# A transformer kernel whose pool of weight buffers is laid from the upper end of the on-chip memory downwards

## The chip, the cores and the metric

The kernel runs on one core of a Trainium2 chip. The metric is the device time in microseconds (us) of one execution; it is measured in several runs, and their median counts. A profile of one more execution shows what each engine did: TensorE (PE, matmuls; its weight loads are shown apart as PEld), VectorE (DVE), ScalarE (ACT), GpSimd (POOL), SyncE (SP, which issues most DMAs) and the DMA engines, which move data between the chip's large memory and the on-chip memory that the engines work from.

## What is computed

The reference takes 256 tokens of width 1024 through three layers: an HGRN2 layer (a gated linear recurrence) and a banded attention layer, each with a SwiGLU feed-forward of width 2816 and with modulation by a conditioning vector, and then a layer with four kinds of attention heads and a convolutional feed-forward of width 4096. Cut to what matters:

```python
c_act = silu(c)
for layer in range(2):
    sh1, sc1, g1, sh2, sc2, g2 = split(c_act @ mod_w[layer] + mod_b[layer], 6)
    u = rms_norm(h, norm_mix[layer]) * (1 + sc1) + sh1
    mix = hgrn2_mixer(u, ...) if layer == 0 else chunk_band_attention(u, k_pad, v_pad, ...)
    h = h + g1 * mix
    u = rms_norm(h, norm_ffn[layer]) * (1 + sc2) + sh2
    h = h + g2 * swiglu(u, ffn_w_in[layer], ffn_w_out[layer])
    if layer == 0:
        k_pad, v_pad = shared_kv(h, c_act, ...)
x = rms_norm(h, final_norm)
h = rms_norm(x, attn_pre_norm)
mix = concat(moba(h), nsa(h), diff(h), swa(h))
x = x + rms_norm(mix @ w_out, attn_post_norm)
x = x + rms_norm(conv_ffn(rms_norm(x, ffn_pre_norm), ...), ffn_post_norm)
```

All of it is in float32, and some 240 MB of weights are each read once. So nearly all the work is large matrices times 256 token columns.

## The kernel before

**Weights.** Every weight matrix is cut into units of at most 128 x 1088 numbers. A unit is loaded by SP into a tile `w_raw` (`emit_dma`, L186; 7 such buffers). The units of the large projections are then split in two: ACT writes the rounded part `w_hi` (L193), and DVE writes the rest `w_lo` = `w_raw` - `w_hi` (L195), 4 buffers each. The conditioning vectors' matrices are used from `w_raw` as they are. All three tiles come from the pool `wts`. `pump` issues each load as soon as the buffer that it needs was read for the last time, so the loads run ahead of the matmuls by up to seven units.

**Matmuls.** The activations are split in the same way into a high and a low tile. `mm3` multiplies high by high, high by low and low by high into one accumulator (L258, L259, L260):

```python
PE.matmul(o, lhsT=whi, rhs=xhi, ...)   # L258
PE.matmul(o, lhsT=whi, rhs=xlo, ...)   # L259
PE.matmul(o, lhsT=wlo, rhs=xhi, ...)   # L260
```

The first operand (`lhsT`, 128 x 128) is loaded into the array ahead of its matmul, and the second (`rhs`) streams through it. In most projections the weights are loaded and 256 columns of activations stream (`lin_A`, `lin_At`, `acc_pairs`). In `lin_B` and `down_B` it is the other way round: the activations are loaded and 512 columns of weights stream. The split activations lie in the eight large slots `s0` to `s7` of the pool `big` (all shown as `s` in the profile), with one exception: the output projection of the first layer (`a_w_out`, 175 to 201 us) reads them from the tiles `ohi` and `olo` of that phase's own pool (`hg_o`, L966, and `hg_ol`, L971). Its 192 matmuls use the same function `acc_pairs` and the same weight tiles as the other output projections.

**Order.** The order of all work is written out by hand (`HG_ORDER`, `L1_ORDER`, `B2_ORDER` and the order of the steps), under `tc.manual_schedule()`.

**Memory.** Tiles get their places from pools that stand one behind the other: `cst` (constants), `big` (the slots), `wts`, `wk` (small work tiles: `sq`, `nt`, `sig`, `rstd`, ...), and behind `wk` one pool for each phase in turn (`hg`, `mid`, `b2`: `ohi`, `olo`, `att`, `pt`, `bias`, ...), the next taking the place of the last:

```python
cst = ctx.enter_context(tc.tile_pool(name="cst", bufs=1))
big = ctx.enter_context(tc.tile_pool(name="big", bufs=1))
wts = ctx.enter_context(tc.tile_pool(name="wts", bufs=1))
wk = ctx.enter_context(tc.tile_pool(name="wk", bufs=2))
```

Of the kernel before, what the change touches and what calls it, by code (L numbers as in the profile page):

```python
# [131 lines left out]
def kernel(ctx: ExitStack, tc: tile.TileContext, x, c, mod_w, mod_b, norm_mix, norm_ffn,  # L132
# [10 lines left out]

    cst = ctx.enter_context(tc.tile_pool(name="cst", bufs=1))
    big = ctx.enter_context(tc.tile_pool(name="big", bufs=1))
    wts = ctx.enter_context(tc.tile_pool(name="wts", bufs=1))
    wk = ctx.enter_context(tc.tile_pool(name="wk", bufs=2))
    phase = {}
    ps = ctx.enter_context(tc.tile_pool(name="ps", bufs=1, space=bass.MemoryType.PSUM))
# [1742 lines left out]
```

## Time and profile before

| what | value |
|---|---|
| median of 3 runs | 1158.81 us (1157.78 to 1161.32) |
| the profiled execution's own time | 1159.24 us |
| its span, from the first to the last instruction | 1157.4 us |
| PE busy / PEld busy | 1116.8 us (96%) / 1035.9 us (89%) |
| DVE / ACT / POOL busy | 763.6 us (66%) / 573.7 us (50%) / 140.0 us (12%) |
| SP's DMA queue, share of 16 DMA engines | 64.3% |

The busy time of PE is a sum of instructions that overlap: a matmul is shown from its start to its modelled end, and the next one starts before that. So what a matmul costs is read from the distance between two starts, not from its duration. The time around the span (1159.24 - 1157.4 us) is not in the profile.

### The profile page before, as it was taken

Reading aid. Unit: us, or ns where it says so; the run is one execution under the profiler, and the core shown is the slowest. Engines: PE = TensorE matmul, PEld = TensorE weight load, DVE = VectorE, ACT = ScalarE, POOL = GpSimd, SP = SyncE. Lnnn points to the kernel's source line nnn. Section 1 sums busy time; section 2 is a strip of 40 time slices with the busy share of each in tenths; the row PEclk is TensorE's granted clock in tenths of the full one; section 3 lists DMA queues with packets and bytes.
Section 4 is the critical chain, followed back from the end, with each engine's and each line's share of the span. In section 5 each row is a group of like instructions: output and inputs, shape, how many; then the busy total and the mean of one; then the engine's idle time right before and its main releaser. Section 6 shows DMA issues by size and latency. Waiting matters only on the chain.

```text
span 1157.4 us, 23598 instructions
## 1 busy us (share of the span) xinstructions
PE 1116.8 (96%) x9689; PEld 1035.9 (89%) x9689; DVE 763.6 (66%) x1237; ACT 573.7 (50%) x913; POOL 140.0 (12%) x201
## 2 busy tenths in 40 slices
PE   6988999999999999999999999999998999999997
PEld 5985789899999979888999999988888999999997
DVE  3586765877777587885564454667766766766666
ACT  3355454644344566565443443746555544544454
POOL 4044410000000001250000000013312100000000
PEclk9989999999999999999999999999999999999999
DMA  9966776888888776865766556673342656555551
GB/s 278 332 236 201 225 227 224 277 285 294 291 282 290 224 239 226 286 238 172 229 194 207 183 172 167 158 217 110 110 146 77 217 181 199 178 180 189 187 178 55
DMA packets 176124, 241.92 MB, mean 209 GB/s; under 512 B 18712, under 2 KB 142160, under 8 KB 176016
## 3 DMA queue, kind: packets, MB, share of 16 engines
q1 hardware_dynamic: 174928, 239.54, 64.3%
q8 instruction: 76, 1.25, 0.4%
q0 software_dynamic: 912, 0.81, 0.3%
q14 instruction: 32, 0.26, 0.1%
q10 hardware_dynamic: 176, 0.07, 0.0%
HBM read 239.33 MB, written 1.05 MB: 208 GB/s over the span
## 4 chain that ended last, share of the span: by engine, by line
PE 83%; DVE 7%; ACT 4%; DMA 3%; issue 2%; POOL 1%; SPq 0%; DVEq 0%; ACTq 0%; POOLq 0%
PE pb_b L258 14%; PE pb_b L260 14%; PE pb_b L259 14%; PE pb_acc L258 10%; PE pb_acc L260 10%; PE pb_acc L259 10%; DVE w_lo L195 2%; ACT w_hi L193 2%; DMA w_raw<-in_kv_w_dram 1%; DMA w_raw<-in_a_w_in_dram 1%; PE pb_b L463 1%; PE pb_b L1216 1%; PE pb_gv L524 1%; DVE nt L573 1%; DMA w_raw<-in_mod_w_dram 1%
## 5 line engine op out<-in xcount | busy, mean ns | idle before, releaser
L195 DVE TENSOR_TENSOR w_lo<-w_raw,w_hi 128x1024 fp32r<-128x1024 f32 (+1 forms) x335 | 409.2, 1245 | 178.2 <-ACT w_hi L193 171.0
L258 PE MATMUL pb_b<-s,w_hi 128*128 128x256 f32 x1488 | 424.7, 285 | 5.1 <-ACT s L1750 2.9
L260 PE MATMUL pb_b<-s,w_lo 128*128 128x256 f32 x1488 | 422.0, 284 | 1.5 <-DVE w_lo L195 1.4
L259 PE MATMUL pb_b<-s,w_hi 128*128 128x256 f32 x1488 | 422.9, 284 | 0.4
L193 ACT CAST w_hi<-w_raw 128x1024 fp32r<-128x1024 f32 (+1 forms) x336 | 342.1, 1045 | 78.9 <-DMA w_raw<-in_a_w_in_dram 16.1
L258 PEld LDWEIGHTS pb_b<-s,w_hi 128*128 128x128 f32 x1488 | 285.9, 192 | 12.5 <-issue 3.8
L260 PEld LDWEIGHTS pb_b<-s,w_lo 128*128 128x128 f32 x1488 | 286.0, 192 | 2.4 <-DVE w_lo L195 2.3
L259 PEld LDWEIGHTS pb_b<-s,w_hi 128*128 128x128 f32 x1488 | 286.0, 192 | 1.9 <-DVE s L585 0.7
L258 PE MATMUL pb_acc<-s,w_hi 128*128 128x256 f32 x656 | 190.4, 290 | 0.2 <-ACT w_hi L193 0.2
L260 PE MATMUL pb_acc<-s,w_lo 128*128 128x256 f32 x656 | 186.9, 285 | 2.8 <-DVE w_lo L195 2.8
L259 PE MATMUL pb_acc<-s,w_hi 128*128 128x256 f32 x656 | 186.6, 284 | 0.0
L258 PEld LDWEIGHTS pb_acc<-s,w_hi 128*128 128x128 f32 x656 | 126.9, 193 | 5.4 <-issue 3.7
L260 PEld LDWEIGHTS pb_acc<-s,w_lo 128*128 128x128 f32 x656 | 126.8, 193 | 3.4 <-DVE w_lo L195 3.4
L259 PEld LDWEIGHTS pb_acc<-s,w_hi 128*128 128x128 f32 x656 | 127.0, 194 | 0.2
L1209 POOL TENSOR_SCALAR att<-att,sm 128x128 f32<-128x128 f32 (+1 forms) x72 | 46.7, 666 | 631.9 <-DVE sm L1202 348.0
L1063 ACT CAST s<-sig 128x512 fp32r<-128x512 f32 x38 | 23.6, 622 | 121.1 <-DVE sig L1073 121.1
L258 PE MATMUL pb_acc<-w_hi,s 128*128 128x512 f32 x192 | 77.4, 403 | 1.7 <-ACT s L579 1.0
L259 PE MATMUL pb_acc<-w_lo,s 128*128 128x512 f32 x192 | 75.6, 394 | 0.8 <-DVE w_lo L195 0.8
L260 PE MATMUL pb_acc<-w_hi,s 128*128 128x512 f32 x192 | 75.5, 393 | 0.0
L1776 ACT ACTIVATE sig<-att,vb_t,vc_t 128x256 f32<-128x256 f32 x32 | 17.6, 596 | 77.4 <-DVE att L1771 77.4
L1069 ACT ACTIVATE sig<-pb_b 128x512 f32<-128x512 f32 x22 | 13.2, 598 | 79.7 <-PE pb_b L260 79.7
L1786 POOL TENSOR_TENSOR sig<-sig,rstd 128x512 f32<-128x512 f32 x16 | 22.7, 1417 | 240.1 <-ACT sig L1784 240.1
(373 smaller groups left out, 1259.2 us busy)
## 6 DMA issues: line engine op xcount, KB each, us to landing
w_raw<-in_mod_w_dram SPq DMA_DIRECT2D x96, 512.0 KB, 4.9
w_raw<-in_ffn_w_in_dram SPq DMA_DIRECT2D x88, 512.0 KB, 5.1
w_raw<-in_ffn_w_out_dram SPq DMA_DIRECT2D x44, 512.0 KB, 4.7
w_raw<-in_a_w_in_dram SPq DMA_DIRECT2D x32, 512.0 KB, 5.2
w_raw<-in_ffn_w_gate_dram SPq DMA_DIRECT2D x32, 512.0 KB, 3.7
w_raw<-in_ffn_w_up_dram SPq DMA_DIRECT2D x32, 512.0 KB, 5.0
w_raw<-in_ffn_w_down_dram SPq DMA_DIRECT2D x32, 512.0 KB, 3.6
w_raw<-in_kv_mod_w_dram SPq DMA_DIRECT2D x16, 512.0 KB, 5.6
```

The costliest lines, as they stand in the source:

```text
L193: SC.copy(hi, raw)
L195: DV.tensor_sub(lo, raw, hi.bitcast(F32))
L258: PE.matmul(o, lhsT=whi, rhs=xhi, start=start, stop=False, skip_group_check=True)
L259: PE.matmul(o, lhsT=whi, rhs=xlo, start=False, stop=False, skip_group_check=True)
L260: PE.matmul(o, lhsT=wlo, rhs=xhi, start=False, stop=stop, skip_group_check=True)
L463: PE.matmul(st[:, 0:256], lhsT=mean_d, rhs=sq[:, 256 * m:256 * m + 256], start=j == 0 and m == 0, stop=j == n - 1 and m == 1)
L524: PE.matmul(g[32 * j:32 * j + 32, 0:256], lhsT=by, rhs=r, start=start, stop=stop, tile_position=(0, 32 * j))
L1063: SC.copy(hi, hid)
L1069: SC.activation(sg, g, AF.Silu)
L1209: GP.tensor_scalar(t[:, i, cs], t[:, i, cs], r[:, 2 * b + i:2 * b + i + 1], 1.0, op0=OP.mult, op1=OP.mult)
L1776: SC.activation(zm, am, AF.Identity, bias=vcol("conv_b")[:, f:f + 1], scale=vc_t[:, 64 + f:65 + f])
L1786: GP.tensor_mul(zp, zp, rs_pair())
```

## The change

The pool `wts` is laid from the upper end of the memory downwards. All other pools stay on the lower side, so `wk` and the phases' pools, which stood behind `wts`, now stand right behind `big`.

```diff
-    wts = ctx.enter_context(tc.tile_pool(name="wts", bufs=1))
+    wts = ctx.enter_context(tc.tile_pool(name="wts", bufs=1, side="right"))
     wk = ctx.enter_context(tc.tile_pool(name="wk", bufs=2))
```

The two built programs have the same instructions in the same order with the same waits on every engine; only addresses differ. These are the addresses (bytes within a partition) and what is left of them after division by 256. A buffer of `wts` is 4352 = 17 x 256 bytes, so all buffers of the pool have the same remainder.

| tile | before | remainder | after | remainder |
|---|---|---|---|---|
| `s0` to `s7` | 30720 to 96256 | 0 | the same | 0 |
| `w_raw`, first of 7 | 96256 | 0 | 164064 | 224 |
| `w_hi`, first of 4 | 126720 | 0 | 194528 | 224 |
| `w_lo`, first of 4 | 144128 | 0 | 211936 | 224 |
| `sq`, first of `wk` | 161536 | 0 | 96256 | 0 |
| `ohi`, first of 4 | 209952 | 32 | 144672 | 32 |
| `olo`, first of 4 | 218144 | 32 | 152864 | 32 |
| `flip` (constant of the bias steps) | 181664 | 160 | 116384 | 160 |
| `late` (constants) | 25440 | 96 | 25440 | 96 |

All tiles of `wk` and of the phases move down by 65280 = 255 x 256 bytes and keep their remainders. The tiles of `wts` move up by 67808 bytes.

## Rows read from the trace of the kernel before

**Rows 1.** The page: busy us, share of the span and instructions of each engine.

```profile
PE 1116.8 (96%) x9689; PEld 1035.9 (89%) x9689; DVE 763.6 (66%) x1237; ACT 573.7 (50%) x913; POOL 140.0 (12%) x201
```

**Rows 2.** The page: the chain of waits that ended last, by engine and by line.

```profile
PE 83%; DVE 7%; ACT 4%; DMA 3%; issue 2%; POOL 1%; SPq 0%; DVEq 0%; ACTq 0%; POOLq 0%
PE pb_b L258 14%; PE pb_b L260 14%; PE pb_b L259 14%; PE pb_acc L258 10%; PE pb_acc L260 10%; PE pb_acc L259 10%; DVE w_lo L195 2%; ACT w_hi L193 2%; DMA w_raw<-in_kv_w_dram 1%; DMA w_raw<-in_a_w_in_dram 1%; PE pb_b L463 1%; PE pb_b L1216 1%; PE pb_gv L524 1%; DVE nt L573 1%; DMA w_raw<-in_mod_w_dram 1%
```

**Rows 3.** The page's costliest groups: xcount, then busy us, mean ns, idle before.

```profile
L258 PE MATMUL pb_b<-s,w_hi 128*128 128x256 f32 x1488 | 424.7, 285 | 5.1 <-ACT s L1750 2.9
L260 PEld LDWEIGHTS pb_b<-s,w_lo 128*128 128x128 f32 x1488 | 286.0, 192 | 2.4 <-DVE w_lo L195 2.3
L258 PE MATMUL pb_acc<-s,w_hi 128*128 128x256 f32 x656 | 190.4, 290 | 0.2 <-ACT w_hi L193 0.2
L259 PE MATMUL pb_acc<-w_lo,s 128*128 128x512 f32 x192 | 75.6, 394 | 0.8 <-DVE w_lo L195 0.8
```

**Rows 4.** Timeline of PE in a SwiGLU round, operand from a slot: start, duration.

```profile
243.73 0.28 PE L259 MATMUL pb_b<-s,w_hi 128*128 128x256 f32 x1
243.85 0.28 PE L260 MATMUL pb_b<-s,w_lo 128*128 128x256 f32 x1
...
246.13 0.28 PE L258 MATMUL pb_b<-s,w_hi 128*128 128x256 f32 x1
```

**Rows 5.** Timeline of PE in the first layer's output projection, operand from `ohi`, `olo`.

```profile
182.32 0.28 PE L258 MATMUL pb_acc<-ohi,w_hi 128*128 128x256 f32 x1
182.44 0.28 PE L259 MATMUL pb_acc<-olo,w_hi 128*128 128x256 f32 x1
...
186.76 0.28 PE L260 MATMUL pb_acc<-ohi,w_lo 128*128 128x256 f32 x1
```

**Rows 6.** Instructions on `ohi`: duration ns min/median/max, first and last start.

```profile
L260 PEld LDWEIGHTS pb_acc<-ohi,w_lo x64: 187/188/189, 175.5 to 200.3; 128*128 128x128 f32 x64
L966 ACT CAST ohi<-s x4: 617/620/624, 160.1 to 185.6; 128x512 fp32r<-128x512 f32 x4
L971 DVE TENSOR_TENSOR olo<-s,ohi x4: 684/685/687, 161.4 to 186.6; 128x512 fp32r<-128x512 f32 x4
```

**Rows 7.** Stretches: busy us of the engines, granted TensorE clock, DMA share, GB/s.

```profile
182.30:186.80 4.50, 4.50 (x41) 4.50 (x40) 3.80 (x6) 2.84 (x4) 0.00 (x0) 1.00 0.57 185
243.70:246.20 2.50, 2.50 (x23) 2.50 (x22) 0.82 (x1) 2.14 (x3) 0.00 (x0) 1.00 1.02 400
30.00:60.00 30.00, 28.89 (x331) 27.58 (x331) 16.50 (x30) 11.81 (x16) 0.00 (x0) 1.00 1.01 337
240.00:270.00 30.00, 30.00 (x254) 29.45 (x253) 21.75 (x27) 12.57 (x16) 0.00 (x0) 1.00 0.92 315
```

**Rows 8.** Timeline of PE in the last feed-forward, 512 columns of weights streaming.

```profile
955.01 0.39 PE L258 MATMUL pb_acc<-w_hi,s 128*128 128x512 f32 x1
...
957.28 0.39 PE L259 MATMUL pb_acc<-w_lo,s 128*128 128x512 f32 x1
```

**Rows 9.** The splits of the hidden activations, from slots: duration ns min/median/max.

```profile
L1063 ACT CAST s<-sig x38: 620/622/627, 221.5 to 1142.2; 128x512 fp32r<-128x512 f32 x38
L1064 DVE TENSOR_TENSOR s<-sig,s x38: 691/693/696, 222.1 to 1142.9; 128x512 fp32r<-128x512 f32 x38
```

**Rows 10.** DMA packets and SP's queue, 64.5 to 65.5 us, then 600 to 603 us.

```profile
DMA packets 87, 0.37 MB, mean 372 GB/s; under 512 B 6, under 2 KB 19, under 8 KB 87
q1 hardware_dynamic: 87, 0.37, 94.4%
...
DMA packets 124, 0.43 MB, mean 145 GB/s; under 512 B 18, under 2 KB 18, under 8 KB 124
q1 hardware_dynamic: 124, 0.43, 37.3%
```

**Rows 11.** Matmuls of the bias steps, `flip` loaded and weights streaming: ns min/median/max.

```profile
L1107 PE MATMUL pb_b<-w_hi,flip x8: 391/393/491, 373.2 to 394.7; 128*128 128x512 f32 x6, 64*128 64x512 f32 x2
```

**Rows 12.** SP's DMA queue over the whole span: packets, MB, share of 16 engines.

```profile
q1 hardware_dynamic: 174928, 239.54, 64.3%
```

## The prediction

> **What bounds the kernel now.** I read the page's busy times first, then the chain of waits, then the costliest groups, and then the timeline of PE inside two of them. PE is busy for 1116.8 us of the span of 1157.4 us, DVE for 763.6 us [rows 1]. The chain of waits agrees: 83% of the span goes through PE, and the three lines of `mm3` hold 14 + 14 + 14% (accumulators `pb_b`) and 10 + 10 + 10% (`pb_acc`), 72% together [rows 2]. DMA ends a wait in 3% of it. So a change counts if it alters the distance between two matmuls, or if it makes something else late.
>
> A place in memory takes no time of its own, and the order, the waits and the number of instructions are the same in both programs. The question is therefore only whether any instruction or transfer runs at another speed when its tile starts at another address. The trace of before can answer a good part of that, because its tiles do not all start alike: the slots and all tiles of `wts` start at multiples of 256 bytes, while `ohi`, `olo` lie 32 bytes past one and `late` 96 bytes.
>
> **The part that I expect to count: the distance between two matmuls.** In a SwiGLU round the streamed operand comes from a slot, and from the start at 243.73 us to the one at 246.13 us there are 20 steps [rows 4]: 2.40 us / 20 = 120.0 ns each. In the first layer's output projection the streamed operand is `ohi` or `olo`, and from 182.32 us to 186.76 us there are 38 steps [rows 5]: 4.44 us / 38 = 116.8 ns. [...] The weight load beside it takes 188 ns in the middle with `ohi` and 192 ns in the mean with a slot [rows 3, 6], though it reads the same `w_lo` buffers. So 3.2 ns a matmul hang on the place of the streamed tile, and the load of the next weights, which runs at the same time, feels it too. My reading, which the trace doesn't prove: two reads that run side by side, one of the streamed tile and one of the next weights, disturb each other most when both start at the same remainder. With `ohi` the two starts are 32 bytes apart (modulo 256), with a slot 0.
>
> How large the disturbance can be follows from the 512-column matmuls: 955.01 to 957.28 us are 10 steps [rows 8], so 227 ns each. 256 columns more cost 227 - 120 = 107 ns, and a matmul of 256 columns thus has 120 - 107 = 13 ns that don't come from its columns. With `ohi` there are 10 of these left.
>
> After the change the slots still start at remainder 0, and `w_hi`, `w_lo` at 224. Streamed start minus weight start is 0 - 224, which is 32 modulo 256: the very distance that `ohi` (32) has from the weights (0) in before. So I take 116.8 ns for all 256-column matmuls that stream from a slot. There are 3 x 1488 + 3 x 656 = 6432 of them [rows 3] (one of the three lines stands there for each; the other two have the same count). All of them together: 6432 x 3.2 ns = 20.6 us. Not all are on the chain: the six lines hold 72% of 1157.4 us = 833 us of it. The 576 512-column matmuls take 576 x 227 ns = 131 us of that and the 192 of `ohi`, `olo` 22 us; the other 680 us are 680 / 0.120 = 5670 matmuls. 5670 x 3.2 ns = 18.1 us.
>
> What is late next: between 240 and 270 us the DMA engines are at 0.92 with PE full [rows 7]; a PE that is 2.7% faster asks them for 0.945, which still fits. Between 30 and 60 us they are at 1.01 with PE at 28.89 of 30 us [rows 7], so PE's gain there is lost: 60 us of the beginning, of which perhaps 40 us are such matmuls, give back 1 us. For the short waits for `w_hi` and `w_lo` between stages (4% of the chain on ACT and 7% on DVE [rows 2]) I take off another 1 us. That leaves -16 us.
>
> **The other parts.** *512 columns of weights streaming:* here the weights stream and the slot's tile is loaded, so the distance is 224 - 0 = -32 modulo 256, which no row shows. By the nearest rows [rows 4, 5] it is between -3.2 and +3.2 ns for 576 matmuls, 1.8 us either way; I take 0. *First layer's output projection:* `ohi` keeps 32 and the weights get 224, a distance of 64; if that is as bad as 0, 192 x 3.2 ns = +0.6 us; I take 0. *ACT and DVE:* a cast into `ohi` takes 620 ns and one into a slot 622 ns; the subtraction on `ohi`, `olo` 685 ns and on slots 693 ns [rows 6, 9]. So nothing is added to L193 and L195, whose two inputs move together anyway. At most it is 8 ns x 335 subtractions = 2.7 us of DVE, which PE covers. *DMA:* the rows of `w_raw` will start 224 past a multiple of 256. `late` does that in before (96 past), and its rows make up most of the second from 64.5 to 65.5 us: 0.944 x 1000 ns x 16 engines / 87 packets = 174 ns for 0.37 MB / 87 = 4.25 KB, 24.5 bytes per ns. Rows of 4 KB into `w_raw` between 600 and 603 us: 0.373 x 3000 x 16 / 124 = 144 ns for 3.47 KB, 24.0 bytes per ns [rows 10]. No cost is seen; I take 0. *Work tiles:* all keep their remainders, so 0.
>
> Sum: the profiled execution took 1159.24 us, and 1159.24 - 16 = 1143.2 us. It stands 0.4 us above the median of the runs, 1158.81 us, so the median after should be near 1143 us.
>
> [...]
>
> **The rivals.** *(a) Nothing changes.* The 3.2 ns may hang on the start or the region of the streamed tile alone and not on its distance from the weights. For it: in before the weights never start anywhere but at remainder 0, so the rows can't part the two. Against it: the weight load, too, is shorter beside `ohi` (188 against 192 ns [rows 3, 6]), so the two reads know of each other. Then only the 512-column matmuls have a moved streamed tile, 1.8 us either way: 1159 us.
>
> [...]
>
> [...]
>
> *(c) Slower, through a worse distance.* Of the split matmuls, only those of the bias steps load weights that start off the multiple in before, `flip` (remainder 160): 393 ns in the middle against 394 ns in the mean with a slot [rows 3, 11], so no sign of harm, but these come in groups of four and never settle. If the new distance cost 3 ns instead of saving 3, it would be 5670 x 3 ns = +17 us: 1176 us.
>
> *(d) More than forecast.* If all of the 13 ns went, 5670 x 13 ns = 74 us: 1085 us. `ohi` speaks against it.
>
> **How the numbers follow.** Forecast 0.58, (a) 0.22, (b) 0.07, (c) 0.08, (d) or anything below the forecast's own range 0.05. The forecast's own range goes from 1159 - 20.6 - 1.8 - 0.6 = 1136 to 1152 us (less than half of the gain is left where other engines take over, or part of the matmuls settle at 120 ns). To leave out no more than 2 in 10, the range must take in (a): 1135 to 1162 us. A measurement of this kernel can tell about 0.3% (3.5 us) from no change. Faster by more than that: 0.58 + 0.05 = 0.63; within it: 0.22; slower: 0.15.
>
> **What would show it.** If the first step is right, the timeline of a SwiGLU round shows steps of 116 to 118 ns in place of 120.0, weight loads of 188 ns and not 192, and the 30 us from 240 us on hold some 260 matmuls where there were 254 [rows 7]. ACT's and DVE's split of a weight unit stay as they are, and 1 KB and 4 KB rows of `w_raw` take as long as before. [...] The forecast is wrong as a whole if the distance matters modulo something larger than 256 bytes, since the two distances are alike only so far.

## The result and the profile after

| | before | after |
|---|---|---|
| median of the runs (us) | 1160.07 (1157.78 to 1161.37) | 1146.71 (1142.66 to 1148.35) |
| the profiled execution's own time (us) | 1159.24 | 1142.66 |
| its span (us) | 1157.4 | 1140.9 |
| ratio after / before, with its 95% interval | | 0.9889 [0.9866, 0.9912] |

The changed kernel is 1.1% faster. The forecast was 1143 us (range 1135 to 1162), so the direction, the size and, as the experiments show, the step that it rested on were right; two smaller terms were not. The profiled execution of after is the fastest of its four, so what is counted in its trace stands nearer to the lower end of the runs than to their median.

The page of after, busy times and the chain of waits by engine, answers to [rows 1, 2]:

```profile
PE 1098.1 (96%) x9689; PEld 1014.4 (89%) x9689; DVE 763.4 (67%) x1237; ACT 573.4 (50%) x913; POOL 138.1 (12%) x201
PE 82%; DVE 6%; DMA 4%; ACT 4%; issue 2%; POOL 1%; SPq 0%; DVEq 0%; ACTq 0%; POOLq 0%
```

DVE and ACT do what they did. PE and its weight loads lost 18.7 and 21.5 us of busy time with the same instructions, and DMA ends 4% of the chain where it ended 3%.

The page's costliest groups of after (xcount, busy us, mean ns), to be held against [rows 3]:

```profile
L258 PE MATMUL pb_b<-s,w_hi 128*128 128x256 f32 x1488 | 419.4, 282 | 5.1 <-ACT s L1750 2.9
L260 PEld LDWEIGHTS pb_b<-s,w_lo 128*128 128x128 f32 x1488 | 280.3, 188 | 2.6 <-DVE w_lo L195 2.6
L258 PE MATMUL pb_acc<-s,w_hi 128*128 128x256 f32 x656 | 186.7, 285 | 0.6 <-ACT w_hi L193 0.6
L259 PE MATMUL pb_acc<-w_lo,s 128*128 128x512 f32 x192 | 76.6, 399 | 0.8 <-DVE w_lo L195 0.8
```

The 256-column matmuls became shorter (285 to 282, 290 to 285 ns), the weight load beside them went from 192 to 188 ns, and the 512-column matmuls became longer (394 to 399 ns).

The timeline of PE in after, in the same SwiGLU feed-forward as [rows 4] (start, duration), then in the last feed-forward, as [rows 8], and in the first layer's output projection, as [rows 5]:

```profile
239.74 0.28 PE L259 MATMUL pb_b<-s,w_hi 128*128 128x256 f32 x1
239.85 0.28 PE L260 MATMUL pb_b<-s,w_lo 128*128 128x256 f32 x1
...
242.07 0.28 PE L258 MATMUL pb_b<-s,w_hi 128*128 128x256 f32 x1
...
954.78 0.40 PE L260 MATMUL pb_acc<-w_hi,s 128*128 128x512 f32 x1
...
956.41 0.40 PE L258 MATMUL pb_acc<-w_hi,s 128*128 128x512 f32 x1
...
180.38 0.28 PE L258 MATMUL pb_acc<-ohi,w_hi 128*128 128x256 f32 x1
...
183.92 0.28 PE L258 MATMUL pb_acc<-ohi,w_hi 128*128 128x256 f32 x1
```

The first stretch has 20 steps in 2.33 us, 116.5 ns each (120.0 before). The second has 7 steps in 1.63 us, 233 ns (227 before). The third has 30 in 3.54 us, 118.0 ns (116.8 before). Over the whole trace the distance between two starts, for all matmuls of one kind and without the long steps at breaks, has these means: 256 columns from a slot 119.9 ns before and 116.8 after, 512 columns 228.4 and 233.2, `ohi` and `olo` 117.0 and 117.5.

Two stretches of after, against [rows 7] (busy us and count of PE, PEld, DVE, ACT, POOL; granted clock; DMA share; GB/s):

```profile
240.00:270.00 30.00, 30.00 (x261) 29.46 (x260) 22.64 (x28) 13.96 (x16) 0.00 (x0) 1.00 0.93 317
30.00:60.00 30.00, 28.80 (x335) 27.50 (x333) 17.10 (x30) 12.21 (x18) 0.00 (x0) 1.00 1.05 322
```

The feed-forward holds 261 matmuls where it held 254. Between 30 and 60 us the DMA engines are full, as before, and move 322 GB/s where they moved 337: here something got dearer.

Where the gain arises is read from the first and last starts of three lines. Before, `L1063` went from 221.5 to 1142.2 us [rows 9] and `L1107` began at 373.2 us [rows 11]. In after (instructions of a line: duration ns, first and last start):

```profile
L1063 ACT CAST s<-sig x38: 618/621/622, 220.3 to 1125.5; 128x512 fp32r<-128x512 f32 x38
L1107 PE MATMUL pb_b<-w_hi,flip x8: 391/394/500, 368.0 to 389.1; 128*128 128x512 f32 x6, 64*128 64x512 f32 x2
L1776 ACT ACTIVATE sig<-att,vb_t,vc_t x32: 585/595/604, 870.5 to 1119.5; 128x256 f32<-128x256 f32 x32
L653 PE MATMUL pb_gv<-w_raw,crep x256: 272/273/423, 9.1 to 51.9; 128*32 128x128 f32 x128
```

and the two of these lines that weren't shown of before:

```profile
L1776 ACT ACTIVATE sig<-att,vb_t,vc_t x32: 587/596/605, 884.8 to 1136.2; 128x256 f32<-128x256 f32 x32
L653 PE MATMUL pb_gv<-w_raw,crep x256: 272/273/423, 9.3 to 50.5; 128*32 128x128 f32 x128
```

After is 1.4 us late at 52 us, 1.2 us early at 220, 5.2 at 368, 14.3 at 870 and 16.7 at the end. So the first 220 us bring next to nothing, the projections and feed-forwards up to 870 us bring 13 us, and the last feed-forward, where 256- and 512-column matmuls take turns, brings 2.4 us in 250.

### The profile page after: what moved, and what is told of

Its sections match the earlier page's. It is cut to its first block, busy times and chain, and to the rows that moved or that the text cites. A ratio compares the mean times of both kernels' runs of the same rounds, so it can differ in the third digit from the quotient of the medians.

```text
span 1140.9 us, 23598 instructions
## 1 busy us (share of the span) xinstructions
PE 1098.1 (96%) x9689; PEld 1014.4 (89%) x9689; DVE 763.4 (67%) x1237; ACT 573.4 (50%) x913; POOL 138.1 (12%) x201
## 4 chain that ended last, share of the span: by engine, by line
PE 82%; DVE 6%; DMA 4%; ACT 4%; issue 2%; POOL 1%; SPq 0%; DVEq 0%; ACTq 0%; POOLq 0%
PE pb_b L258 14%; PE pb_b L260 14%; PE pb_b L259 14%; PE pb_acc L258 11%; PE pb_acc L260 10%; PE pb_acc L259 10%; DVE w_lo L195 2%; DMA w_raw<-in_a_w_in_dram 2%; ACT w_hi L193 2%; PE pb_b L463 1%; PE pb_b L1216 1%; DMA w_raw<-in_mod_w_dram 1%; DMA w_raw<-in_kv_w_dram 1%; PE pb_gv L524 1%; DVE nt L573 1%
## 5 line engine op out<-in xcount | busy, mean ns | idle before, releaser
L258 PE MATMUL pb_b<-s,w_hi 128*128 128x256 f32 x1488 | 419.4, 282 | 5.1 <-ACT s L1750 2.9
L260 PE MATMUL pb_b<-s,w_lo 128*128 128x256 f32 x1488 | 416.2, 280 | 1.6 <-DVE w_lo L195 1.5
L259 PE MATMUL pb_b<-s,w_hi 128*128 128x256 f32 x1488 | 417.3, 280 | 0.3
L258 PEld LDWEIGHTS pb_b<-s,w_hi 128*128 128x128 f32 x1488 | 280.3, 188 | 12.7 <-issue 4.0
L260 PEld LDWEIGHTS pb_b<-s,w_lo 128*128 128x128 f32 x1488 | 280.3, 188 | 2.6 <-DVE w_lo L195 2.6
L259 PEld LDWEIGHTS pb_b<-s,w_hi 128*128 128x128 f32 x1488 | 280.3, 188 | 1.9 <-DVE s L585 0.7
L260 PE MATMUL pb_acc<-s,w_lo 128*128 128x256 f32 x656 | 183.4, 280 | 4.0 <-DVE w_lo L195 4.0
L258 PE MATMUL pb_acc<-s,w_hi 128*128 128x256 f32 x656 | 186.7, 285 | 0.6 <-ACT w_hi L193 0.6
L259 PE MATMUL pb_acc<-s,w_hi 128*128 128x256 f32 x656 | 183.1, 279 | 0.0
L258 PEld LDWEIGHTS pb_acc<-s,w_hi 128*128 128x128 f32 x656 | 123.3, 188 | 5.8 <-issue 3.5
L260 PEld LDWEIGHTS pb_acc<-s,w_lo 128*128 128x128 f32 x656 | 123.3, 188 | 4.8 <-DVE w_lo L195 4.8
L259 PEld LDWEIGHTS pb_acc<-s,w_hi 128*128 128x128 f32 x656 | 123.4, 188 | 0.2
L1063 ACT CAST s<-sig 128x512 fp32r<-128x512 f32 x38 | 23.6, 621 | 115.9 <-DVE sig L1073 115.9
L258 PE MATMUL pb_acc<-w_hi,s 128*128 128x512 f32 x192 | 78.3, 408 | 1.7 <-ACT s L579 1.0
L260 PE MATMUL pb_acc<-w_hi,s 128*128 128x512 f32 x192 | 76.5, 399 | 0.0
```

The lines of the kernel that those rows point to most:

```text
L258: PE.matmul(o, lhsT=whi, rhs=xhi, start=start, stop=False, skip_group_check=True)
L259: PE.matmul(o, lhsT=whi, rhs=xlo, start=False, stop=False, skip_group_check=True)
L260: PE.matmul(o, lhsT=wlo, rhs=xhi, start=False, stop=stop, skip_group_check=True)
L1063: SC.copy(hi, hid)
```

## The experiments

Names: S is the start of the streamed tile and W the start of the tile that is loaded beside it, each modulo 256 bytes. With 256 columns S is the slots' (0) or that of `ohi` and `olo`, and W that of `w_hi`, `w_lo`; with 512 columns it is the other way round. Spare tiles shift the line numbers of some kernels by two or three (L258 becomes L260). Three theories were to be told apart. The **distance** theory is that of the prediction: W - S counts. The **place** theory: only W counts. The **region** theory: it is the upper part of the memory that is faster. Means of steps come from the trace, sorted by the addresses of the built program. Runs of one kernel lie up to 8 us apart, so the time of a kernel that was run once (experiments 3, 4, 7, 8, 11 and 12) is a weak sign; its steps are read instead.

**1. The upper end with the old remainders.**

```diff
+    pad = ctx.enter_context(tc.tile_pool(name="pad", bufs=1, side="right"))
+    pad.tile([P, 56], F32, name="padt")
     wts = ctx.enter_context(tc.tile_pool(name="wts", bufs=1, side="right"))
...
-    cst.tile([P, 72], F32, name="gap")
+    cst.tile([P, 8], F32, name="gap")
```

> The weight pool stays at the upper end, but a spare tile of 224 bytes above it puts w_raw, w_hi and w_lo back on multiples of 256 (the spare tile gap is cut by 256 bytes to make room, so all other tiles keep their remainders). Distance theory (what counts is the start of the streamed tile minus the start of the weights, modulo 256): 256-column matmuls go back to 120.0 ns, 512-column ones from 233 to 227 ns, early 512-byte rows from 32 to 27 ns; time of before, 1158 to 1161 us. Place theory (the remainder of the weights alone counts): the same numbers. Region theory (the upper part of the memory, not the remainder, is what helps): 116.8 ns stay, about 1146 us.

Measured: 1159.55 us, ratio 1.0002 [0.9991, 1.0014]. The steps are 119.9 and 228.5 ns. The page's groups:

```profile
L261 PE MATMUL pb_b<-s,w_hi 128*128 128x256 f32 x1488 | 423.5, 285 | 0.3
L262 PEld LDWEIGHTS pb_b<-s,w_lo 128*128 128x128 f32 x1488 | 286.5, 193 | 2.5 <-DVE w_lo L197 2.3
```

Everything of before is back, the 285 ns and the weight load (193 ns, 192 in before). The region theory falls: the whole gain hangs on the remainder.

**2. `w_raw` alone at 0.** `w_raw` gets a pool of its own below a spare tile of 224 bytes.

```diff
+    pad = ctx.enter_context(tc.tile_pool(name="pad", bufs=1, side="right"))
+    pad.tile([P, 56], F32, name="padt")
+    raws = ctx.enter_context(tc.tile_pool(name="raws", bufs=1, side="right"))
...
-        u.raw = wts.tile([P, UNIT], F32, name="w_raw", tag="w_raw", bufs=RAW_BUFS)[:, :u.k * u.w]
+        u.raw = raws.tile([P, UNIT], F32, name="w_raw", tag="w_raw", bufs=RAW_BUFS)[:, :u.k * u.w]
...
-    cst.tile([P, 72], F32, name="gap")
+    cst.tile([P, 8], F32, name="gap")
```

> As after, but w_raw alone back on a multiple of 256; w_hi and w_lo stay at remainder 224. All theories of the matmuls: about 117 ns and 233 ns as in after. If the start of the rows is what makes small packets dearer in the first 60 us: 512-byte rows fall from 32 to 27 ns, the stretch from 30 to 60 us has the DMA share 1.01 of before and not 1.05, and the 1.2 us that after is late at 37 us are gone; the end is then 1 to 2 us earlier than after (1144.5 to 1146 us), or the same if the loads that follow made up for it anyway (the matmuls at 92 us stood 1.7 us earlier in after than in before). If rows' starts cost nothing and it is a matter of a faster PE asking for more: 32 ns and 1146.7 us as in after.

Measured: 1147.45 us, ratio 0.9902 [0.9878, 0.9925], not to be told from after. SP's queue from 44 to 45 us, nearly all rows of 512 bytes (packets, MB, share of 16 engines), in before, in after and here:

```profile
q1 hardware_dynamic: 633, 0.32, 107.5%
```
```profile
q1 hardware_dynamic: 577, 0.29, 116.4%
```
```profile
q1 hardware_dynamic: 568, 0.28, 99.2%
```

1.075 x 1000 ns x 16 / 633 = 27.2 ns a packet before, 32.3 ns in after, 27.9 ns here. So rows of 512 bytes do cost 5 ns more when they are written 224 bytes past a multiple of 256. The conditioning matrices, which arrive in such rows, show what it is worth:

```profile
L656 PE MATMUL pb_gv<-w_raw,crep x256: 272/273/423, 9.3 to 50.6; 128*32 128x128 f32 x128
```

The last of these matmuls starts at 50.6 us (50.5 before, 51.9 in after): 1.3 us are won back. At the end of the program nothing of it can be seen, but these runs can't tell: the granted clock between 60 and 90 us was 0.94 here and 1.00 in after, by 92 us after is ahead again, and the four runs of either kernel lie 6 us apart.

**3. and 4. Eight remainders in one kernel.** Each `w_hi` and `w_lo` buffer is 32 bytes longer, once with the slots at 0, once at 32.

```diff
-        hi = wts.tile([P, UNIT], F32R, name="w_hi", tag="w_hi", bufs=WT_BUFS)[:, :n]
-        lo = wts.tile([P, UNIT], F32R, name="w_lo", tag="w_lo", bufs=WT_BUFS)[:, :n]
+        hi = wts.tile([P, UNIT + 8], F32R, name="w_hi", tag="w_hi", bufs=WT_BUFS)[:, :n]
+        lo = wts.tile([P, UNIT + 8], F32R, name="w_lo", tag="w_lo", bufs=WT_BUFS)[:, :n]
...
-    cst.tile([P, 72], F32, name="gap")
+    cst.tile([P, 8], F32, name="gap")
```

(16 in place of 8 for the slots at 32.)

> As after, but each buffer of w_hi and w_lo is 32 bytes longer, so the four of w_hi start at remainders 224, 0, 32, 64 and the four of w_lo at 96, 128, 160, 192; the slots stay at 0. Distance theory modulo 256, and place theory: 120 ns only beside the w_hi buffer at 0, 117 ns beside the seven others; if the pattern repeats every 64 bytes, 120 ns beside 0, 64, 128 and 192, thus near half of all, and a time near 1153 us; modulo 128: 0 and 128. For 512 columns (weights stream, the slot's tile at 0 is loaded): 227 ns with the streamed buffer at 0 and 233 ns elsewhere, or 227 ns at all multiples of 64. If the region alone counted: 117 ns everywhere.

> The same eight starts of w_hi and w_lo as in the ladder with the slots at 0, but all tiles of the lower side, the slots among them, stand 32 bytes higher, so the slots are at remainder 32. Distance theory: 120 ns moves along, to the w_hi buffer at 32 (modulo 256), or to 32, 96, 160, 224 (modulo 64). Place theory: 120 ns stays with the buffer at 0 (or 0, 64, 128, 192). A theory by which the streamed tile on a multiple of 64 or 256 is needed for the slow case: 117 ns everywhere, about 1143 us if 512 columns take 227 ns, 1147 us if 233 ns.

Measured: 1153.79 and 1149.59 us. Mean steps (ns) of 256-column matmuls from a slot, sorted by W - S modulo 256:

```
W - S           0      32     64     96    128    160    192    224
slots at 0    118.9  118.2  114.9  118.0  119.3  118.1  114.1  118.5
slots at 32   119.1  118.1  117.0  118.1  119.4  118.6  115.8  118.7
```

The two rows have the same shape, though each value stands at another W: the buffer at 224 has 118.5 ns with the slots at 0 and 115.8 with the slots at 32. The place theory falls. New is that 0 and 128 are both bad and 64 and 192 both good. The expectation that 117 ns stand everywhere but at 0 was wrong. So was the one for 512 columns, 227 ns beside one buffer and 233 beside the rest: with the slots at 0 the eight buffers have 229.6 to 233.8 ns (45 to 87 steps each), and the one at distance 0 has 231.8.

**5. and 6. Weights at 192 and at 64.** As after, with a spare tile `pad.tile([P, 8], ...)` or `pad.tile([P, 40], ...)` above the pool, the latter with the smaller `gap`.

> As after, with a spare tile of 32 bytes above the pool, so w_raw, w_hi and w_lo start at remainder 192 in place of 224; nothing else moves. In the ladder with the slots at 0, 256-column matmuls beside weights at 192 took 114.1 ns in the mean (113 in the middle), at 64 114.9, at 0 and 128 near 119; with the slots at 32 the low values moved to 96 and 224. Distance theory with a period of 128 bytes (cheapest where the two starts are 64 apart, dearest where they are 0 apart): 113 to 114 ns in nearly all of them, so some 3 ns under after on 5670 matmuls of the chain, 17 us; 512-column ones at 226 to 229 ns (233 in after), 2 to 4 us; together 1126 to 1129 us, up to 1135 us where ACT or DVE become late. If the ladder's 114 ns came from the mixing of buffers: 117 ns or so, 1143 to 1147 us.

> The same with weights at remainder 64 (spare tile of 160 bytes, gap cut by 256 bytes). Distance theory with a period of 128 bytes: like remainder 192, 113 to 115 ns, 1126 to 1131 us. With a period of 256 and the sign counting: unlike 192, near the 117 ns of after, 1143 to 1147 us.

Measured: 1148.63 us, ratio 0.9910 [0.9889, 0.9932] at 192, and 1136.79 us, ratio 0.9813 [0.9784, 0.9843] at 64. So the steps at 64 are much as expected (114.4 ns; 229.7 ns for 512 columns, with 226 to 229 expected), though the time stands 6 us above its range of 1126 to 1131 us. At 192 they have 116.7 ns in the mean and 233.3 ns, nearer to the second expectation (117 ns) than to the 114 of the ladder. What happens there is seen in the timeline of the run at 192, where side matmuls of other shapes break into the stream:

```profile
265.56 0.28 PE L260 MATMUL pb_b<-s,w_hi 128*128 128x256 f32 x1
265.68 0.28 PE L261 MATMUL pb_b<-s,w_hi 128*128 128x256 f32 x1
265.80 0.28 PE L262 MATMUL pb_b<-s,w_lo 128*128 128x256 f32 x1
...
266.26 0.39 PE L526 MATMUL pb_b<-lq,ones 128*32 128x256 f32 x2
266.58 0.39 PE L260 MATMUL pb_b<-s,w_hi 128*128 128x256 f32 x1
...
267.03 0.28 PE L260 MATMUL pb_b<-s,w_hi 128*128 128x256 f32 x1
267.14 0.28 PE L261 MATMUL pb_b<-s,w_hi 128*128 128x256 f32 x1
267.25 0.28 PE L262 MATMUL pb_b<-s,w_lo 128*128 128x256 f32 x1
```

Ahead of the break the steps read 118 118 117 118 118 118 in the trace's nanoseconds, a pattern that repeats; behind it they read 113 113 114 again and again, until a break at 303 us. So the stream of loads and matmuls locks into a repeating pattern, one distance can have more than one of them, and the pattern behind a break can be another than ahead of it. At 64 as at 192 the patterns have means of 113.3 and 117.8 ns. Of the groups of 12 consecutive steps, about 62 in 100 lie at 113 ns and 16 at 118 in the kernel at 64, but 22 and 61 in the one at 192 (the others hold a break or a change).

**7. Weights at 128.** `pad.tile([P, 24], ...)` and the smaller `gap`.

> The same with weights at remainder 128 (spare tile of 96 bytes, gap cut by 256 bytes). Distance theory with a period of 128 bytes: 120.0 ns as in before although the starts are 128 apart, some 1160 us. With a period of 256 bytes, as the prediction took it: farthest from the bad distance, so 117 ns or less, 1146 us or less.

Measured: 1156.95 us, 118.9 ns in the mean, with patterns of 118.6 and 120.0 ns; 512 columns 232.4 ns. The distance of 128, farthest from 0, is nearly as bad as 0. It is not the same, though: the weight load takes 189 ns, not 193:

```profile
L261 PE MATMUL pb_b<-s,w_hi 128*128 128x256 f32 x1488 | 420.7, 283 | 0.3
L262 PEld LDWEIGHTS pb_b<-s,w_lo 128*128 128x128 f32 x1488 | 280.7, 189 | 2.3 <-DVE w_lo L197 2.3
```

**8. Finer steps.** As after with weights from 160 on and an offset inside the buffer that changes from unit to unit.

```diff
+    pad = ctx.enter_context(tc.tile_pool(name="pad", bufs=1, side="right"))
+    pad.tile([P, 16], F32, name="padt")
...
+        j = state["conv_w"] % 4
+        oh, ol = (2 + 2 * j, 10 + 2 * j) if n + 16 <= UNIT else (0, 0)
-        hi = wts.tile([P, UNIT], F32R, name="w_hi", tag="w_hi", bufs=WT_BUFS)[:, :n]
-        lo = wts.tile([P, UNIT], F32R, name="w_lo", tag="w_lo", bufs=WT_BUFS)[:, :n]
+        hi = wts.tile([P, UNIT], F32R, name="w_hi", tag="w_hi", bufs=WT_BUFS)[:, oh:oh + n]
+        lo = wts.tile([P, UNIT], F32R, name="w_lo", tag="w_lo", bufs=WT_BUFS)[:, ol:ol + n]
```

> Finer steps around remainder 192: units that are at most 1072 numbers long are written into their w_hi and w_lo buffers with an offset that changes from unit to unit, so w_hi starts at 168, 176, 184, 192 and w_lo at 200, 208, 216, 224 (w_raw at 160; slots at 0). If the distance counts in whole steps of 32 or 64 bytes: 192 to 216 alike (near 114 ns) and 168 to 184 alike (near 118 ns), with a jump. If it counts continuously: lowest at 192, rising to both sides.

Measured: 1157.65 us. The means in ns: 168 119.1, 176 117.3, 184 118.4, 192 118.2, 200 118.7, 208 116.8, 216 118.1, 224 116.8. Neither expectation holds. 192 stands at 118.2 here and at 114.1 in the ladder, so a buffer's step does not hang on its own distance alone. That its neighbours in the stream count, as a locked pattern would have it, fits this but was not tried apart. Nothing finer than 32 bytes follows from this run.

**9. The old side with 64 bytes ahead of the weights.**

```diff
+    pad = ctx.enter_context(tc.tile_pool(name="pad", bufs=1))
+    pad.tile([P, 16], F32, name="padt")
     wts = ctx.enter_context(tc.tile_pool(name="wts", bufs=1))
```

> The kernel before, pool of weights on the lower side as it was, with a spare tile of 64 bytes ahead of it: w_raw, w_hi, w_lo start at remainder 64, everything behind them moves up by 64 bytes, the slots stay at 0. Distance theory (slots 0, weights 64): steps of 113.3 ns with stretches of 117.8 ns, 512 columns 229 to 230 ns, a time like that of the run with weights at 64 at the upper end, 1133 to 1141 us, without any use of the upper end. If the upper end has a part in it (the region, or the work tiles' move): nearer to before, 1146 to 1159 us.

Measured: 1131.99 us, ratio 0.9759 [0.9735, 0.9784]: faster than both kernels and 1 us under the range expected, with one tile of 64 bytes and without the change. The timeline, 20 steps in 2.27 us, 113.5 ns each, and a stretch of 30 us:

```profile
600.02 0.28 PE L261 MATMUL pb_acc<-s,w_hi 128*128 128x256 f32 x1
...
602.29 0.28 PE L260 MATMUL pb_acc<-s,w_hi 128*128 128x256 f32 x1
```
```profile
600.00:630.00 30.00, 30.00 (x268) 29.46 (x267) 17.04 (x18) 14.30 (x17) 0.00 (x0) 1.00 0.64 211
```

The same 30 us hold 252 matmuls in before and 259 in after. The time is 4.8 us under that of the same distance at the upper end (experiment 6). With runs of 1126.8 to 1133.6 us here and 1132.6 to 1140.8 there, that is less than the spread of either. In the two profiles, 8.0 us apart, 5.2 of them have arisen by 150 us. The first 30 us of experiment 6, then of this kernel, then of experiments 5 and 10:

```profile
0.00:30.00 30.00, 18.42 (x180) 14.21 (x180) 9.03 (x27) 9.01 (x21) 12.95 (x28) 0.89 1.00 272
```
```profile
0.00:30.00 30.00, 18.78 (x183) 14.17 (x184) 10.14 (x28) 10.31 (x23) 12.85 (x28) 1.00 1.00 276
```

```profile
0.00:30.00 30.00, 18.63 (x181) 14.02 (x181) 9.84 (x28) 10.00 (x22) 12.85 (x28) 1.00 1.02 279
```
```profile
0.00:30.00 30.00, 19.95 (x192) 15.64 (x193) 11.18 (x29) 11.35 (x23) 12.85 (x28) 0.89 0.94 280
```

In experiment 6 the mean granted clock is 0.89 against 1.00 here. But that does not decide how far PE comes: experiment 10 has 0.89 too and 192 matmuls, experiment 5 has 1.00 and 181. What goes with the count is where `w_raw` starts. The four profiled kernels with `w_raw` on a multiple of 256 (before, experiments 1, 2 and 10) have 191 to 195 matmuls in these 30 us, and all others, at whatever clock, 180 to 186. Experiments 6 and 9 both have it off the multiple, so what makes the gap between the two stays open.

**10. 64 bytes inside the buffers, for 256 columns only.** The kernel before, where 512-column units keep their remainder 0 (`wide`).

```diff
+        self.wide = w == 512
...
+        o = 0 if u.wide or n + 16 > UNIT else 16
-        hi = wts.tile([P, UNIT], F32R, name="w_hi", tag="w_hi", bufs=WT_BUFS)[:, :n]
-        lo = wts.tile([P, UNIT], F32R, name="w_lo", tag="w_lo", bufs=WT_BUFS)[:, :n]
+        hi = wts.tile([P, UNIT], F32R, name="w_hi", tag="w_hi", bufs=WT_BUFS)[:, o:o + n]
+        lo = wts.tile([P, UNIT], F32R, name="w_lo", tag="w_lo", bufs=WT_BUFS)[:, o:o + n]
...
+            u.wide = down.__name__ == "down_B"
...
```

> The kernel before with all pools in their old places; w_hi and w_lo are written 64 bytes behind their buffers' start, so at remainder 64, for the units beside which 256 columns stream, and at 0 for those of lin_B, the 512-wide first projections and the last down projection. Distance theory: 256 columns as with weights at 64 (113.3 and 117.8 ns), 512 columns back from 229.7 ns to the 228.4 of before, early 512-byte rows at 27 ns: 1 to 2 us under the run with weights at 64, some 1132 to 1139 us. If the alternation of two remainders in the last feed-forward unsettles the pattern, its 256-column steps come out at 116 to 119 ns there and the time at 1140 to 1146 us.

Measured: 1133.14 us, ratio 0.9777 [0.9759, 0.9796]. The 512-column steps are back at 228.4 ns and the rows of 512 bytes at 27 ns, as expected. But the 256-column steps at distance 64 are at 115.9 ns in the mean, not 114.3: about 30 groups in 100 lie at 113 ns and 48 at 118. From 221 to 373 us they have 113.5 ns; from 885 us on, in the last feed-forward, they have 117.5, which is what the second expectation gave for that stage. So in this execution the patterns took back what the two terms gave. It is the slowest of this kernel's five, though (1138.20 us), and the profiled one of experiment 9 the fastest of its four (1126.84 us); by their medians the two kernels end level.

**11. Weights at 192 once more**, the same kernel.

> The kernel with weights at 192 once more. In its first profile the steps stood at 117.8 ns in most stretches and at 113.3 ns in others (267 to 303, 341 to 372, 546 to 639 us), and the level changed only at single long steps of 203 to 224 ns. If the level that follows such a break is a matter of chance: other stretches at 113.3 ns, another share of them. If it is fixed by the program's order and places: the same stretches within a few. 1144 to 1153 us either way.

Measured: 1149.49 us. The stretch from 600 to 630 us, in the first profile and in this one:

```profile
600.00:630.00 30.00, 30.00 (x267) 30.00 (x266) 15.52 (x17) 12.56 (x15) 0.00 (x0) 1.00 0.69 222
```
```profile
600.00:630.00 30.00, 30.00 (x257) 30.00 (x257) 14.50 (x16) 11.29 (x14) 0.00 (x0) 1.00 0.67 217
```

The same program has 267 matmuls there once and 257 the other time. Some stretches were alike in both (341 to 372 us at 113.3 ns), others not (546 to 639 us only in the first). So in these two executions the pattern that follows a break was the same in some places and not in others. What decides it stays open.

**12. Weights at 32.** `pad.tile([P, 48], ...)` and the smaller `gap`.

> Weights at remainder 32 (spare tile of 192 bytes at the upper end, gap cut by 256 bytes), slots at 0: the same 32 bytes as in after, with the other sign (weights ahead of the slots' remainder). If the sign doesn't count, as the prediction assumed: 116.7 ns and 512 columns at 233 ns, 1143 to 1148 us. If it counts, other levels than 116.7; by the ladder, where 32 stood at 118.2 and 224 at 118.5 ns among changing buffers, not more than 118 ns, 1150 us or less.

Measured: 1155.58 us; 256 columns 118.3 ns, 512 columns 233.2 ns. Step and time stand above the bounds that were expected (118 ns, 1150 us). So the sign counts: 32 bytes behind the slots' remainder gave 116.8 ns, 32 bytes ahead 118.3. This kernel also holds the cleanest proof of the distance, since `ohi`, `olo` and the weights now both stand at 32:

```profile
L262 PEld LDWEIGHTS pb_acc<-ohi,w_lo x64: 187/192/192, 176.7 to 202.0; 128*128 128x128 f32 x64
```
```profile
184.32 0.28 PE L260 MATMUL pb_acc<-ohi,w_hi 128*128 128x256 f32 x1
...
186.72 0.28 PE L262 MATMUL pb_acc<-ohi,w_lo 128*128 128x256 f32 x1
```

20 steps in 2.40 us are 120.0 ns, and the load takes 192 ns: what the slots had in before, at a place that is no multiple of 256.

All kernels with one fixed distance together, steps of 256 columns (mean ns), with the matmuls of `ohi` and `olo` as a second, independent set:

```
W - S   slots (S, W)                          ohi, olo (S, W)
  0     119.9 before, exp. 1 (0, 0)           119.8 exp. 12 (32, 32)
 32     118.3 exp. 12 (0, 32)                 118.3 exp. 6 (32, 64)
 64     114.3 exp. 9, 114.4 exp. 6 (0, 64)
 96                                           118.0 exp. 7 (32, 128)
128     118.9 exp. 7 (0, 128)
160                                           119.9 exp. 5 (32, 192)
192     116.7 exp. 5, 117.4 exp. 11 (0, 192)  117.5 after (32, 224)
224     116.8 after, 117.0 exp. 2 (0, 224)    117.0 before (32, 0), 116.7 exp. 9 (96, 64)
```

Wherever a distance occurs in this table with two different S, the values agree within 1 ns. Between the two ladders, where the distance changes from buffer to buffer, they differ by up to 2 ns (114.9 and 117.0 at 64).

## Why the prediction was right, and where it was not

**The 256-column step: right in mechanism and size.** Forecast 120.0 to 116.8 ns, measured 119.9 to 116.8, with the weight load at 188 for 192 ns and 261 matmuls in 30 us. The two stretches of before from which the forecast took its 3.2 ns can be compared: shape (128 x 256) and granted clock (1.00) are the same in both [rows 4, 5, 7]. Counted stage by stage, with 3.1 ns won on each 256-column step from a slot and 4.8 ns lost on each 512-column one, it explains the starts that were compared above:

```
stretch of before (us)   256 columns   512 columns   won by the sum   won by the starts
0 to 221.5                   661            88            1.6              1.2
221.5 to 373.2              1234             0            3.8              4.0
373.2 to 884.8              3118           108            9.1              9.1
884.8 to 1136.2             1435           333            2.9              2.4
```

So nearly all of the 256-column matmuls counted (6448 here, some more than the 6432 of the two groups that the forecast read), not the 5670 of the forecast: 17.4 us by the sum, 16.7 by the starts.

That the first row of the table agrees is luck. After is 1.1 us late at 60 us and 1.8 us early at 92 us, though only some 155 such steps, 0.5 us, lie between. In this stretch the two executions were granted another clock (before, then after):

```profile
60.00:90.00 30.00, 25.78 (x425) 24.58 (x424) 22.82 (x48) 15.31 (x21) 13.71 (x21) 0.89 0.64 216
```
```profile
60.00:90.00 30.00, 25.47 (x440) 23.97 (x440) 24.80 (x51) 17.95 (x25) 14.61 (x22) 1.00 0.71 234
```

A granted clock of 0.89 over 30 us can have cost before at most 0.11 x 30 us = 3.3 us, an estimate from the first of these rows. The other three rows of the table stand on firmer ground: from 221.5 us on the mean granted clock is 1.00 in both, and 15.5 of the 16.7 us are won there.

That it is the distance, and that after has the very distance that `ohi` had in before, is shown by experiments 1, 3, 4 and 12. What the two reads share, so that their distance counts, is not shown. Rival (a) fell with the first timeline of after, (c) and (d) with it. The prediction's caution that two equal remainders modulo 256 might not be enough was not needed. But its picture, "most when both start at the same remainder" and easier elsewhere, is too simple: 128 (118.9 ns) and 160 (119.9) are nearly or just as bad, and the best distance is 64, which no row of before showed. For 512 columns it is even the other way round: of the kernels with one fixed distance, those with equal starts have the shortest step (228.4 ns). So the forecast of 116.8 ns came out because the trace held a row with the very same distance, sign included, not because of that picture.

Experiment 1 and after differ by 224 bytes (modulo 256) in the start of the weights, while all other tiles keep their remainders, and by 3.1 ns a matmul (119.9 and 116.8 ns). So for these split float32 matmuls the place of the weights counts, even where the streamed tile keeps its remainder.

**512 columns: the mis-sized term.** Taken as 0 with bounds of 1.8 us. It measured 233.2 - 228.4 = 4.8 ns on 576 matmuls, 2.8 us, beyond the bound. The bound was taken from 256-column rows (3.2 ns), and there was no reason why a longer stream should feel no more than a short one. Experiments 9 and 10 show the same step at 229.5 and 228.4 ns.

**The first layer's output projection: right.** 117.0 to 117.5 ns, 192 x 0.5 = 0.1 us, within the 0 to 0.6 us given.

**DMA: wrong in the nearest row, small in effect.** The step took 0 from `late` and looked at rows of 4 KB. Rows of 1 KB (46 ns from 30 us on) and 4 KB (159 ns) indeed kept their time, by their medians over most of the span, in before and after alike, but rows of 512 bytes went from 27 to 32 ns (experiment 2). Between 60 and 72 us even the rows of 4 KB had a median of 165 ns in after. Before has 159 there, as have experiments 1, 2 and 10, with `w_raw` on the multiple. In before every row of `w_raw` starts on a multiple, and the rows of `late`, of 5 KB, say nothing of short ones. Rival (b), slower through the loads and given 0.07, thus has a part of the truth: a cost of the loads is there, 5 ns on the rows of 512 bytes of the first 60 us and 6 ns on those of 4 KB for some 12 us behind them, and none on rows of 4 KB from 72 us on. It put the program 1.4 us back at 52 us; what is left of that at the end can't be told. Why a row is dearer at such a start is not shown.

**The sum.** Forecast -16 us; the two profiled executions differ by 1159.24 - 1142.66 = 16.6 us, the medians by 13.4. That the profiled executions come so near to the forecast is in part luck, since its misses partly cancel: it counted some 780 matmuls too few (2.4 us), took off 2 us for the start and the waits, where the starts show less than 1 (17.4 against 16.7 us), and lacked the 512-column loss (529 x 4.8 ns = 2.5 us in the stretches counted). Its 1143 us stands 3.7 us below the median of after. The other three runs of after, 1145.4 to 1148.4 us, left no trace, so why they are slower is not known; experiment 11 shows that two executions of one program can differ in their patterns.

## What to carry to other kernels

Look at the distance between the starts of the two tiles that TensorE reads at once, not only at their sizes: in this kernel the whole gain of a new memory layout came from 32 bytes, and a spare tile of 64 bytes in the old layout gave twice as much (ratio 0.9759 against 0.9889). Read the distance between two matmul starts to the nanosecond in each stage; where two stages with the same shapes differ, compare the addresses of their operands. Which distance is good has to be measured for each shape: the one that was worst with 256 columns here was best with 512 (distance 0: 119.9 and 228.4 ns). Where a price is needed for a case that the trace doesn't show, take the row of the same size, not only of the same kind.

## What the runs showed of the hardware

- The step of back-to-back split float32 matmuls (128 x 128 loaded, 256 columns streaming) depends on W - S modulo 256, sign included: 119.9 ns at 0, 118.3 at 32, 114.3 at 64 (115.9 in experiment 10), 118.9 at 128, 116.7 to 117.4 at 192, 116.8 at 224. At 512 columns it went from 228.4 ns (both at 0) to between 229.5 and 233.3.
- The stream locks into repeating patterns of a few steps (120 throughout at 0; 120 113 116 117 and 116 117 117 at 224; 113 113 114 at 64), and one distance can have two of unlike mean (113.3 and 117.8 ns at 64 and 192). Behind a break by other matmuls the pattern can be another, not always alike in two executions: 267 and 257 matmuls in the same 30 us of the same program.
- Rows of 512 bytes written into the on-chip memory took 27 to 28 ns where they started on a multiple of 256 bytes and 32 ns at 224; rows of 4 KB took 159 and 165 ns (medians) between 60 and 72 us, and 159 ns in both cases from then on. In the first 30 us the kernels with `w_raw` on the multiple came to 191 to 195 matmuls, the others to 180 to 186, with granted clocks of 0.89 and 1.00 in both groups.
